# A fixed order from the z products into the SSD chunks, and an opening with two loads moved and one rounding on another engine

## The chip, the core and the metric

The kernel runs on one NeuronCore of a Trainium2 chip. The core has TensorE (PE, the matmuls), VectorE (DVE), ScalarE (ACT), GpSimd (POOL) and SyncE (SP, which here only issues DMA transfers). Each engine takes its own instructions in the order in which they stand in its queue, and waits on semaphores for the others. Data lie in SBUF, matmul results in eight PSUM banks. The metric is the device time of one execution, in microseconds (us); lower is better.

## What is computed

One layer of a hybrid encoder over 1024 tokens of width 1024, all in float32 (cut from the reference):

```
h = rmsnorm(x, norm_mix_w) * (1 + sc_m) + sh_m          # sc_m, sh_m, ... = c_act @ w_ada + b_ada
z, xbc, dt_raw, q, k, v = split(h @ w_in)
xbc = silu(causal_dwconv(xbc) + b);  xs, bm, cm = split(xbc)
dt = softplus(dt_raw + dt_bias);  A = -exp(a_log)
y_ssd = ssd_scan(xs * dt, dt * A, bm, cm) + d_skip * xs  # 8 heads, states carried over chunks
y_ssd = rmsnorm(y_ssd * silu(z), ssd_norm_w)
y_att = chunk_attention(q, k, v, rel_bias)
x = x + g_m * (concat[y_ssd, y_att] @ w_out)
h = rmsnorm(x, norm_ffn_w) * (1 + sc_f) + sh_f
x = x + g_f * ((silu(g) * v) @ w_down)                   # g, v = causal_dwconv(h @ w_up)
out = rmsnorm(x, final_norm_w)
```

## The kernel before

Every float32 operand of a large product is split into a high part, rounded to the matmul's format, and a low part, the rest: `split` writes the high part on ACT and the low part on DVE (lines 80 to 86). A product is then three matmuls, high by high, high by low and low by high (`mm3`, lines 75 to 78).

**Who sets the order.** The program text gives dependences; a planner that simulates the timeline puts the instructions of each engine in an order and assigns buffers. Three things bind it. `tc.issue_after(i)` puts an instruction behind `i` on its engine. `InOrder` (line 43) wraps VectorE, ScalarE and TensorE as `V`, `A` and `T`: while `.on` is set, each instruction goes behind the one before it, in program order. `pe` (line 683) chains TensorE's instructions of the SSD in the same way. GpSimd and the DMA queue are not wrapped.

**The opening** (lines 264 to 348). SP issues four x tiles of 128 tokens (line 267). `norm1` squares a tile on ACT, takes the root on POOL and scales it on DVE. For each of eight blocks `kt` of the model width, `mod_col` (line 131) loads a block of `w_ada` twice, for the scale and the shift, and reduces it on DVE (line 134). TensorE transposes the block of four x tiles (line 327), ACT applies scale and shift (line 249, tile `hf`), and `h_block` takes the high part (line 250) and the low part (line 251) on DVE. Products with the first columns of `w_in` follow (`first_qk`, `first_v`). The four x tiles of the second half come later, in blocks 3 to 6.

**The z products** (lines 731 to 770). z and `dt_raw` are computed in two halves of 260 columns, `ch` 1 and then 0. A half has four weight chunks of two blocks each (`wz_weights`, tiles `wzh` and `wzl`; four buffers, so that a chunk of the second half is split when the first half has left its buffer, and the last two chunks are loaded after the first two are split). Per token tile `st`, `z_tile` does 24 matmuls into a PSUM bank and evacuates it with a tanh on ACT (line 643) and a product on DVE (line 644). Tiles 0 and 1 of each four use the single banks `acc` and `pv`, tiles 2 and 3 the two-bank tiles `s`.

Beside the second half stand `dt_prep` (dt, then cumulative sums on TensorE, line 673), the splits of the output projection's weights (`wout_split`, eight slots, behind the two instructions in `pin`), and `ssd_pre(0)`, the preparation of the first SSD chunk: `xdt` and `xdd` (x times dt, lines 694 and 695), `rm` (lines 701 to 707), the segment sums `sg` on TensorE, `cb` (line 720), and the decay masks, called `th` in the trace (lines 726 and 727).

**The SSD chunks** (lines 921 to 934). The PSUM pools of the z stage are closed and new ones opened over the same eight banks. Per chunk `c` of 128 tokens, `ssd_y` issues `ydp`, `yop` (not in chunk 0) and `stp` on TensorE, `ssd_turn` transposes the y of the chunk before, `ssd_pre` prepares the next chunk, and `wout_half` does half of the output projection of a token tile (tile `wops`, with the left operand `yhl`). Everything on TensorE stands in the order of the text.

Of the kernel before, what the change touches and what calls it, by code (L numbers as in the profile page):

```python
# [64 lines left out]
def tile_block(ctx: ExitStack, tc: tile.TileContext, x, crep, pk, w_ada, w_first, w_ft, w_z,  # L65
# [182 lines left out]
    def h_block(tps, a, b, kt, hi, lo, tmp):  # L248
        i = A.activation(tmp, tps, AF.Identity, scale=a[:, kt:kt + 1], bias=b[:, kt:kt + 1])
        V.tensor_copy(hi, c4(tmp))  # L250
        return i.ins, V.tensor_tensor(lo, c4(tmp), f32(hi), ALU.subtract).ins
# [12 lines left out]
    for p in (0, 1):  # L264
        new_pair(p)
    for st in range(4):
        nc.sync.dma_start(xts[st], x[st * P:(st + 1) * P, :])

# [9 lines left out]
    adw = wu.tile([P, 2, 1024], F32, tag="w2", bufs=1, name="adat2")  # L278
# [24 lines left out]
    for hh in range(2):  # L303
# [7 lines left out]
        for kt in range(KT):  # L311
            if hh == 0:
                mod_col(SC_M + kt, wu.tile([P, 1024], F32, tag="wh", name="adat"))
                mod_scale(amix, SC_M, NMIX, kt)
                mod_col(SH_M + kt, adw[:, kt % 2, :])
                mod_shift(bmix, SH_M, kt)
                t = raw_tile(768)
                nc.sync.dma_start(t, w_first[kt])
                split(wsh[:, kt, :], ws_lo(kt), t, A, V)
                for st in range(4, NT):  # L320
                    if XL[st - 4] == kt:
                        V.tensor_copy(xts[st][:, 0:1], amix[:, kt:kt + 1])
                        nc.sync.dma_start(xts[st], x[st * P:(st + 1) * P, :])
                        norm1(st)
            tps = tp_.pop() if tp_ else ps0.tile([P, 512], F32, tag="tp0", bufs=2, name="tp0")
            for j in range(4):
                T.transpose(tps[:, j * P:(j + 1) * P], xts[4 * hh + j][:, kt * P:(kt + 1) * P], ident)
            tmp = s0.tile([P, 512], F32, tag="hf", bufs=2, name="hf")
            hi, lo = ht(hh, kt)
            pin_ = h_block(tps, amix, bmix, kt, hi, lo, tmp)  # L330
            if kt == split_at - 1:
                hpin = pin_
# [270 lines left out]
    def wout_split(slot, t):  # L603
        dh, j = WORDER[slot]
        h, l = (n[slot // 4][:, slot % 4].rearrange("p a b -> p (a b)") for n in (hth, htl))
        with tc.issue_after(pin[0]), tc.issue_after(pin[1]):
            if j < 2:
                split(h, l, t, A, V)
            else:
                for b in range(2):  # L610
                    c = slice(512 * b, 512 * b + 512)
                    k = SNW + order[2 * j + b]
                    split(h[:, c], l[:, c], t[:, c], A, V, scale=pkt[:, k:k + 1])
        ws[dh] += [(h[:, k:k + 512], l[:, k:k + 512]) for k in (0, 512)]
# [17 lines left out]
    def z_tile(ch, st, wz):  # L632
        if st % 4 < 2:
            ps = psv.tile([P, 512], F32, tag=("acc", "pv")[st % 4], bufs=1, name="zps")[:, 0:260]
        else:
            ps = s_tile()[:, 0:260]
        for kt in range(KT):
            mm3(ps, hth[st // 4][:, st % 4, kt, :], htl[st // 4][:, st % 4, kt, :],
                wz[kt // 2][0][:, kt % 2, :],
                wz[kt // 2][1][:, kt % 2, :], kt == 0, kt == KT - 1)  # L640
        nz = 260
# [4 lines left out]
        if ch == 1:  # L646
            V.scalar_tensor_tensor(zs[:, st, 512:520], ps[:, 252:260], 2.0,
                                   pkt[:, DTB:DTB + 8], op0=ALU.mult, op1=ALU.add)

    def dt_prep():  # L650
# [19 lines left out]
        pin[:] = [i.ins for i in split(adh, adl, sm["adt"], A, V)]  # L670
# [19 lines left out]
    def ssd_pre(c, xp_, sgp_, between=None):  # L690
        cs = slice(c * P, (c + 1) * P)
# [3 lines left out]
        G.tensor_tensor(h8(xdd), h8(xdt), hb("de", c), ALU.mult)  # L695
        ms_ = []
        for g in range(2):
            rm = bcp.tile([P, 2, 4, P], F32R, tag="rm", bufs=2, name="rm")
            hs = slice(c * 8 + 4 * g, c * 8 + 4 * g + 4)
            for h in range(4):  # L700
                A.activation(rm[:, 0, h, :], tle, AF.Copy, scale=f32(adh)[:, hs.start + h:hs.start + h + 1])
            if g == 0:
                V.tensor_tensor(rm[:, 1], tle.unsqueeze(1).to_broadcast([P, 4, P]),
                                f32(adl)[:, hs].unsqueeze(2).to_broadcast([P, 4, P]), ALU.mult)
            else:
                for h in range(4):
                    A.activation(rm[:, 1, h, :], tle, AF.Copy,
                                 scale=f32(adl)[:, hs.start + h:hs.start + h + 1])
            sg = sgp_()
            for i in range(2):  # L710
                pe(T.matmul, sg, sgtr, rm[:, i].rearrange("p h l -> p (h l)"), start=i == 0, stop=i == 1)
            if g == 0:
                cbp = xp_()
                for i in range(2):
                    pe(T.matmul, cbp[:, i * P:(i + 1) * P], bt_[i][:, cs], ct_[i][:, cs],
                       start=True, stop=True)
                for i in range(2):
                    pe(T.transpose, cbp[:, (2 + i) * P:(3 + i) * P], bt_[i][:, cs], ident)
                cb = bcp.tile([P, 4, P], F32, tag="cb", bufs=1, name="cb")
                V.tensor_tensor(cb.rearrange("p (a b) l -> p a b l", a=2),  # L720
                                cbp.rearrange("p (a b l) -> p a b l", a=2, b=2),
                                tle1.unsqueeze(2).to_broadcast([P, 2, 2, P]), ALU.mult)
                if between:
                    between()
            m = th512().rearrange("p (h l) -> p h l", h=4)
            pin1 = A.activation(m, sg.rearrange("p (h l) -> p h l", h=4), AF.Exp)
            pin2 = V.tensor_tensor(m, m, cb[:, g:g + 1, :].to_broadcast([P, 4, P]), ALU.mult)
            ms_.append(m)
        pin[:] = [pin1.ins, pin2.ins]
# [26 lines left out]
    for st in range(NT):  # L756
        z_tile(0, st, wz)
        if st == 0:
            wout_fold(wt[5])
            dt_prep()  # L760
        if st == 3:
            for j in (0, 1, 2):
                wout_split(j, wt[j])
            wout_get(3, 6, 7)
            pre0 = ssd_pre(0, tp_tile, tp_tile)
            wout_split(3, wt[3])
        if st >= 4:
            wout_split(st, wt[st])
# [730 lines left out]
```

## Time and profile before

| | us |
|---|---|
| median of three runs | 1224.24 |
| the runs | 1222.4, 1224.24, 1224.29 |
| the profiled execution | 1223.35 |
| its span, first to last instruction | 1221.6 |
| mean granted TensorE clock | 0.989 |

The profile is taken from one execution. In its timeline a line gives the start (us from the span's start), the duration, the engine, the program line, the operation, what it writes and reads, the shapes, the count of merged instructions, and in brackets the idle time of the engine before it with what ended that. Matmuls overlap, so their spacing is read from the starts. The granted clock is TensorE's, as a share of full speed. A wait for several semaphores is put down to the one that came last.

### The profile page before, as it was taken

How to read it: one execution, taken by the hardware profiler on the slowest of the kernel's cores; microseconds unless marked ns; L12 is line 12 of the kernel's file. 1: busy time of each engine (PE TensorE's matmuls, PEld its weight loads, DVE VectorE, ACT ScalarE, POOL GpSimd, SP SyncE). 2: the span in 40 equal slices, each digit the busy share in tenths (PEclk: the TensorE clock that was granted, in tenths of full speed). 3: DMA queues.
4: the chain of work that ended last, by engine and by line, in shares of the span. 5: the costliest groups of instructions: out<-in, count | busy, mean ns of one | idle time of the engine just before them, and what ended most of it. 6: DMA issues, size and time to landing. Idle time of an engine off the chain costs nothing.

```text
span 1221.6 us, 15652 instructions
## 1 busy us (share of the span) xinstructions
PE 1162.5 (95%) x5802; PEld 977.8 (80%) x5802; DVE 945.3 (77%) x1421; ACT 590.4 (48%) x993; POOL 198.3 (16%) x174
## 2 busy tenths in 40 slices
PE   5999999989999789999899999999999999999995
PEld 3887888778889778888688888888888888888884
DVE  7856555598797858746899988988889869766976
ACT  4537465663333646676454443444434445433443
POOL 1209373682210124300000000000000000000002
PEclk9999999999999989999999999999999999999998
DMA  9632121323554201141123223232232277733533
GB/s 341 249 94 82 36 74 39 128 89 118 175 171 169 91 9 44 53 146 61 69 78 129 94 105 129 90 100 95 104 129 97 90 280 281 270 114 125 169 119 137
DMA packets 56683, 151.91 MB, mean 124 GB/s; under 512 B 5664, under 2 KB 5792, under 8 KB 55200
## 3 DMA queue, kind: packets, MB, share of 16 engines
q1 hardware_dynamic: 49552, 126.54, 31.0%
q10 hardware_dynamic: 7056, 24.38, 5.0%
q8 instruction: 45, 0.74, 0.3%
q14 instruction: 30, 0.25, 0.1%
HBM read 117.61 MB, written 29.10 MB: 120 GB/s over the span
## 4 chain that ended last, share of the span: by engine, by line
PE 81%; DVE 11%; ACT 3%; DMA 2%; issue 2%; POOL 0%; SPq 0%; DVEq 0%; POOLq 0%; ACTq 0%
PE wops L686 6%; PE dn L77 6%; PE dn L76 6%; PE dn L78 6%; PE uY L76 5%; PE uY L78 5%; PE uY L77 5%; PE uZ L78 3%; PE uZ L76 3%; PE uZ L77 3%; PE uX L78 3%; PE uX L76 3%; PE uX L77 3%; PE acc L76 2%; PE acc L77 2%; PE acc L78 2%
## 5 line engine op out<-in xcount | busy, mean ns | idle before, releaser
L918 POOL TENSOR_TENSOR st<-st,mhalf 128x1 f32<-128x1 f32 x16 | 12.7, 799 | 691.9 <-DVE st L917 680.5
L76 PE MATMUL dn<-w 128*128 128x512 f32 x308 | 111.9, 389 | 0.0
L77 PE MATMUL dn<-w 128*128 128x512 f32 x308 | 111.9, 389 | 0.0
L78 PE MATMUL dn<-w 128*128 128x512 f32 x308 | 103.3, 389 | 0.0
L76 PE MATMUL uY<-tH,w 128*128 128x512 f32 x256 | 99.7, 389 | 1.8 <-ACT w L58 1.8
L401 POOL TENSOR_SCALAR p<-p,st 128x640 f32<-128x640 f32 (+4 forms) x64 | 98.8, 1562 | 14.4 <-DVE st L400 9.7
L77 PE MATMUL uY<-tL,w 128*128 128x512 f32 x256 | 99.6, 389 | 0.0
L78 PE MATMUL uY<-tH,w 128*128 128x512 f32 x256 | 99.6, 389 | 0.0
L85 ACT ACTIVATE w<-ya 128x1024 fp32r<-128x1024 f32 (+1 forms) x41 | 39.1, 954 | 84.8 <-PE uY L78 80.8
L686 PE MATMUL wops<-hH,yhl 128*128 128x512 f32 x224 | 74.8, 402 | 3.5 <-DVE yhl L86 2.1
L76 PEld LDWEIGHTS dn<-w 128*128 128x128 f32 x308 | 57.8, 188 | 12.1
L78 PEld LDWEIGHTS dn<-w 128*128 128x128 f32 x308 | 57.8, 188 | 12.0
L77 PEld LDWEIGHTS dn<-w 128*128 128x128 f32 x308 | 57.8, 188 | 11.9
L395 DVE CUSTOM_DVE_ANT_0 p<-s,bias 128x640 f32<-128x640 f32 (+4 forms) x64 | 40.6, 649 | 25.3 <-PE s L383 11.0
L86 DVE TENSOR_TENSOR pt<-tp,pt 128x512 fp32r<-128x512 f32 (+2 forms) x72 | 41.6, 595 | 22.2 <-ACT pt L85 13.5
L76 PEld LDWEIGHTS uY<-tH,w 128*128 128x128 f32 x256 | 48.0, 188 | 12.1 <-ACT w L58 2.2
L77 PEld LDWEIGHTS uY<-tL,w 128*128 128x128 f32 x256 | 48.0, 188 | 10.0
L78 PEld LDWEIGHTS uY<-tH,w 128*128 128x128 f32 x256 | 48.1, 188 | 10.0
L85 ACT ACTIVATE pt<-tp 128x512 fp32r<-128x512 f32 (+2 forms) x72 | 36.3, 523 | 38.8 <-PE pv L438 16.6
L85 ACT ACTIVATE w<-xs 128x1024 fp32r<-128x1024 f32 (+1 forms) x41 | 39.0, 952 | 32.4 <-PE uY L78 32.4
L686 PEld LDWEIGHTS wops<-hH,yhl 128*128 128x128 f32 x224 | 42.4, 190 | 12.8 <-DVE yhl L86 2.5
L76 PE MATMUL s<-hH,wh 128*128 128x512 f32 x128 | 50.5, 394 | 1.2 <-DVE ct L506 1.1
(445 smaller groups left out, 3427.1 us busy)
## 6 DMA issues: line engine op xcount, KB each, us to landing
gz<-a ACTq DMA_DIRECT2D x10, 1024.0 KB, 5.3
wos<-in_w_ada_dram SPq DMA_DIRECT2D x18, 512.0 KB, 4.0
ya<-in_w_up_dram SPq DMA_DIRECT2D x11, 768.0 KB, 4.2
xs<-in_w_up_dram SPq DMA_DIRECT2D x11, 768.0 KB, 4.3
adat<-in_w_ada_dram SPq DMA_DIRECT2D x16, 512.0 KB, 5.8
raws<-in_w_ft_dram SPq DMA_DIRECT2D x16, 512.0 KB, 3.6
qk<-in_w_ada_dram SPq DMA_DIRECT2D x14, 512.0 KB, 4.7
gy<-a ACTq DMA_DIRECT2D x10, 512.0 KB, 2.6
```

Source lines behind the costliest of these rows:

```text
L76: T.matmul(ps, lh, rh, start=start, stop=False, skip_group_check=more)
L77: T.matmul(ps, lh, rl, start=False, stop=False, skip_group_check=more)
L78: T.matmul(ps, ll, rh, start=False, stop=stop, skip_group_check=more)
L85: i = A.activation(hi, src, AF.Copy) if ehi is A else ehi.tensor_copy(hi, src)
L86: return i, elo.tensor_tensor(lo, src, f32(hi), ALU.subtract)
L395: V.tensor_tensor_reduce(out=dst, in0=src, in1=bsl, scale=-1.0, scalar=3e38, op0=ALU.add, op1=ALU.min, accum_out=nm)
L401: G.tensor_scalar(pv_, pv_, rr, None, op0=ALU.mult)
L686: i = op(*a, **k)
L918: G.tensor_tensor(r, ms, mhalf[:, 0:1], ALU.pow)
```

## The change

There are two parts. In the opening, the first scale and shift blocks of `w_ada` are loaded between the second and the third x tile. For the first half of the tokens the high part of h is written by ACT and no longer by DVE. The reduction of the second scale block goes behind the first low part on DVE.

In the second half of the z products `V`, `A` and `T` are set to program order, and the text is an order written by hand: a z tile's matmuls, its evacuation, and pieces of `dt_prep` (now with a separate `dt_sums`), `ssd_pre(0)` (cut into `pre_x`, `pre_rm`, `pre_sg`, `pre_cb` and `pre_m`) and `wout_split` between them. `wout_split` loses its tie to `pin`. `pre_x` and `pre_rm` of chunk 1 are written there too. Tiles 0 and 1 of each four now use `s`, tiles 2 and 3 `acc` and `pv`, in both halves. `T.on` lasts to the last z tile, whose last matmul heads the SSD's chain; `V.on` and `A.on` last through `ssd_y` of chunk 0.

```diff
-    def mod_col(ft, t, at=None):
-        nc.sync.dma_start(t, w_ada[ft])
+    def mod_col(ft, t, at=None, loaded=False):
+        if not loaded:
+            nc.sync.dma_start(t, w_ada[ft])
...
-    def h_block(tps, a, b, kt, hi, lo, tmp):
+    def h_block(tps, a, b, kt, hi, lo, tmp, ehi):
         i = A.activation(tmp, tps, AF.Identity, scale=a[:, kt:kt + 1], bias=b[:, kt:kt + 1])
-        V.tensor_copy(hi, c4(tmp))
+        if ehi is A:
+            i = A.activation(hi, c4(tmp), AF.Copy)
+        else:
+            V.tensor_copy(hi, c4(tmp))
         return i.ins, V.tensor_tensor(lo, c4(tmp), f32(hi), ALU.subtract).ins
...
     for st in range(4):
         nc.sync.dma_start(xts[st], x[st * P:(st + 1) * P, :])
+        if st == 1:
+            nc.sync.dma_start(ad0[0], w_ada[SC_M])
+            nc.sync.dma_start(ad0[1], w_ada[SH_M])
...
-                mod_col(SC_M + kt, wu.tile([P, 1024], F32, tag="wh", name="adat"))
+                t = wu.tile([P, 1024], F32, tag="wh", name="adat") if kt else ad0[0]
+                mod_col(SC_M + kt, t, low[1] if kt == 1 else None, loaded=kt == 0)
...
-                mod_col(SH_M + kt, adw[:, kt % 2, :])
+                mod_col(SH_M + kt, adw[:, kt % 2, :], loaded=kt == 0)
...
-            pin_ = h_block(tps, amix, bmix, kt, hi, lo, tmp)
+            low = h_block(tps, amix, bmix, kt, hi, lo, tmp, (A, V)[hh])
...
-    def z_tile(ch, st, wz):
-        if st % 4 < 2:
-            ps = psv.tile([P, 512], F32, tag=("acc", "pv")[st % 4], bufs=1, name="zps")[:, 0:260]
+    def z_mm(ch, st, wz):
+        if st % 4 > 1:
+            ps = psv.tile([P, 512], F32, tag=("acc", "pv")[st % 4 - 2], bufs=1, name="zps")[:, 0:260]
         else:
             ps = s_tile()[:, 0:260]
...
+    def pre_rm(c, g):
+        rm = bcp.tile([P, 2, 4, P], F32R, tag="rm", bufs=2, name="rm")
+        hs = slice(c * 8 + 4 * g, c * 8 + 4 * g + 4)
+        for h in range(4):
+            A.activation(rm[:, 0, h, :], tle, AF.Copy, scale=f32(adh)[:, hs.start + h:hs.start + h + 1])
+        if g == 0:
+            V.tensor_tensor(rm[:, 1], tle.unsqueeze(1).to_broadcast([P, 4, P]),
+                            f32(adl)[:, hs].unsqueeze(2).to_broadcast([P, 4, P]), ALU.mult)
+        else:
+            for h in range(4):
+                A.activation(rm[:, 1, h, :], tle, AF.Copy,
+                             scale=f32(adl)[:, hs.start + h:hs.start + h + 1])
+        return rm
...
-    for st in range(NT):
-        z_tile(0, st, wz)
-        if st == 0:
-            wout_fold(wt[5])
-            dt_prep()
-        if st == 3:
-            for j in (0, 1, 2):
-                wout_split(j, wt[j])
-            wout_get(3, 6, 7)
-            pre0 = ssd_pre(0, tp_tile, tp_tile)
-            wout_split(3, wt[3])
-        if st >= 4:
-            wout_split(st, wt[st])
+    V.on = A.on = T.on = True
+    V.last = A.last = T.last = None
+    zp = z_mm(0, 0, wz)
+    dt_prep()
+    z_evac(0, 0, zp)
+    zp = z_mm(0, 1, wz)
+    r0 = pre_rm(0, 0)
+    dt_sums()
+    x0 = pre_x(0)
+    z_evac(0, 1, zp)
+    wout_split(0, wt[0])
+    zp = z_mm(0, 2, wz)
+    r1 = pre_rm(0, 1)
+    g0 = pre_sg(r0, tp_tile())
+    z_evac(0, 2, zp)
+    zp = z_mm(0, 3, wz)
+    cb = pre_cb(0, tp_tile())
+    m0 = pre_m(0, g0, cb)
+    wout_fold(wt[5])
+    wout_split(1, wt[1])
+    z_evac(0, 3, zp)
+    zp = z_mm(0, 4, wz)
+    g1 = pre_sg(r1, tp_tile())
+    wout_split(2, wt[2])
+    wout_get(3, 6, 7)
+    m1 = pre_m(1, g1, cb)
+    pre0 = *x0, cb, [m0, m1]
+    z_evac(0, 4, zp)
+    zp = z_mm(0, 5, wz)
+    pre1 = {g: pre_rm(1, g) for g in range(2)}
+    pre1["x"] = pre_x(1)
+    z_evac(0, 5, zp)
+    zp = z_mm(0, 6, wz)
+    wout_split(3, wt[3])
+    wout_split(4, wt[4])
+    z_evac(0, 6, zp)
+    zp = z_mm(0, 7, wz)
+    wout_split(5, wt[5])
+    z_evac(0, 7, zp)
+    for j in (6, 7):
+        wout_split(j, wt[j])
...
     pre, turn = pre0, None
-    chain[:] = [None]
+    T.on = False
+    chain[:] = [T.last]
     for c in range(NT):
         y = ssd_y(c, *pre)
+        V.on = A.on = False
...
-            pre = ssd_pre(c + 1, x_tile, sg_tile, lambda: wout_half(c, slice(0, 3)))
+            pre = ssd_pre(c + 1, x_tile, sg_tile, lambda: wout_half(c, slice(0, 3)),
+                          pre1 if c == 0 else None)
```

More of the change, by code (lines that the diff above doesn't have):

```diff
@@ L605, in wout_split @@
         h, l = (n[slot // 4][:, slot % 4].rearrange("p a b -> p (a b)") for n in (hth, htl))
[L606 to L613, printed above, removed]
+        if j < 2:
+            split(h, l, t, A, V)
+        else:
+            for b in range(2):
+                c = slice(512 * b, 512 * b + 512)
+                k = SNW + order[2 * j + b]
+                split(h[:, c], l[:, c], t[:, c], A, V, scale=pkt[:, k:k + 1])
         ws[dh] += [(h[:, k:k + 512], l[:, k:k + 512]) for k in (0, 512)]
@@ L669, in dt_prep, with dt_sums @@
                                na.unsqueeze(1).to_broadcast([P, 8, 8]), op0=ALU.mult, op1=ALU.mult)
-        pin[:] = [i.ins for i in split(adh, adl, sm["adt"], A, V)]
+        split(adh, adl, sm["adt"], A, V)
+    def dt_sums():
         dps = tp_tile()
@@ new lines, in pre_sg, with pre_cb @@
+    def pre_sg(rm, sg):
+        for i in range(2):
+            pe(T.matmul, sg, sgtr, rm[:, i].rearrange("p h l -> p (h l)"), start=i == 0, stop=i == 1)
+        return sg
+    def pre_cb(c, cbp):
+        cs = slice(c * P, (c + 1) * P)
+        for i in range(2):
+            pe(T.matmul, cbp[:, i * P:(i + 1) * P], bt_[i][:, cs], ct_[i][:, cs],
+               start=True, stop=True)
+        for i in range(2):
+            pe(T.transpose, cbp[:, (2 + i) * P:(3 + i) * P], bt_[i][:, cs], ident)
+        cb = bcp.tile([P, 4, P], F32, tag="cb", bufs=1, name="cb")
+        V.tensor_tensor(cb.rearrange("p (a b) l -> p a b l", a=2),
+                        cbp.rearrange("p (a b l) -> p a b l", a=2, b=2),
+                        tle1.unsqueeze(2).to_broadcast([P, 2, 2, P]), ALU.mult)
+        return cb
@@ L696, in ssd_pre, with pre_m @@
+    def pre_m(g, sg, cb):
+        m = th512().rearrange("p (h l) -> p h l", h=4)
+        pin1 = A.activation(m, sg.rearrange("p (h l) -> p h l", h=4), AF.Exp)
+        pin2 = V.tensor_tensor(m, m, cb[:, g:g + 1, :].to_broadcast([P, 4, P]), ALU.mult)
+        pin[:] = [pin1.ins, pin2.ins]
+        return m
+    def ssd_pre(c, xp_, sgp_, between=None, early=None):
+        xdt, xdd = early["x"] if early else pre_x(c)
         ms_ = []
         for g in range(2):
-            rm = bcp.tile([P, 2, 4, P], F32R, tag="rm", bufs=2, name="rm")
@@ L709, in ssd_pre @@
[L709 to L722, printed above, removed]
+                cb = pre_cb(c, xp_())
```

30 lines of the change are left out of this document (12 added, 18 removed).

## The prediction

> **What bounds the kernel now.** I read the page's busy shares first, then TensorE's waits, then busy time by stretch, then the timeline on both sides of the longest wait.
>
> ```profile
> PE 1162.5 (95%) x5802; PEld 977.8 (80%) x5802; DVE 945.3 (77%) x1421; ACT 590.4 (48%) x993; POOL 198.3 (16%) x174
> ...
> PE ydp L686 <- DVE zs L644: 6.5, 1, 6.5
> ```
>
> TensorE (PE) is the bound over the whole span; only the places where it waits can be won. The longest single wait behind the opening is 6.5 us, ahead of the first SSD product (`ydp`), put down to the evacuation of the last z tile on VectorE (DVE).
>
> ```profile
> 395.10:420.60 25.50, 25.49 (x210) 25.09 (x208) 20.28 (x42) 16.14 (x39) 2.54 (x3) 1.00 0.39 125
> 420.60:427.07 6.47, 0.00 (x0) 0.00 (x0) 6.42 (x9) 5.39 (x15) 2.55 (x2) 0.67 0.00 0
> 427.07:440.00 12.93, 12.93 (x57) 11.37 (x58) 5.16 (x7) 6.04 (x18) 3.70 (x4) 0.77 0.00 1
> ...
> 427.07 3.68 PE L686 MATMUL ydp<-xdt,th 128*128 128x64 f32 x16 [6.48 <-DVE zs L644]
> 439.77 1.89 PE L686 MATMUL ydp<-xdt,th 128*128 128x64 f32 x16
> ...
> 426.61 0.41 DVE L644 SCALAR_TENSOR_TENSOR zs<-zt,s 128x260 f32<-128x260 f32 x1
> ```
>
> The first three rows are stretches: length, then PE, weight loads, DVE, ScalarE (ACT) and POOL busy (instructions), granted clock, DMA share, GB/s. In the second half of the z products PE works 25.49 of 25.50 us. Then it stands still while DVE works on (6.42 of 6.47), and behind that the granted clock is 0.77, so chunk 0 takes 12.70 us (427.07 to 439.77). DVE does the weight splits of the output projection before the last two evacuations; PE needs only the evacuations.
>
> **The z products to chunk 1, part by part.** What chunk 0 costs at full clock follows from a later chunk:
>
> ```profile
> 456.50 1.89 PE L686 MATMUL ydp<-xdt,th 128*128 128x64 f32 x16
> 458.23 1.08 PE L686 MATMUL yop<-state,ct 128*128 128x256 f32 x4
> 459.15 1.03 PE L686 MATMUL stp<-xdd,cb 128*128 128x256 f32 x4
> 460.01 0.60 PE L686 MATMUL xps<-ident,yy 128*128 128x128 f32 x4
> 460.37 0.70 PE L686 MATMUL sg<-rm,sgtr 128*128 128x512 f32 x2
> ...
> 467.50 0.66 PE L686 MATMUL ydp<-xdt,th 128*128 128x64 f32 x5
> ```
>
> Chunk 2 lasts 467.50 - 456.50 = 11.00 us. Chunk 0 has neither the `yop` product (459.15 - 458.23 = 0.92) nor the turn of an earlier y (460.37 - 460.01 = 0.36): 9.72 us.
>
> The change moves the z stage's PE work and adds none: 25.50 us. What it removes is the cover of one wait. `z_mm(0, 0)` is now in program order, while its last weights come late:
>
> ```profile
> 395.10 0.40 PE L76 MATMUL zps<-wzh,hH 128*128 128x260 f32 x2
> ...
> 397.16 0.64 ACT L82 ACTIVATE wzh<-raws 128x520 fp32r<-128x520 f32 x1 [1.48 <-DMA raws<-in_w_z_dram]
> ...
> 399.02 0.70 DVE L83 SCALAR_TENSOR_TENSOR wzl<-raws,wzh 128x520 fp32r<-128x520 f32 x1 [0.38 <-ACT wzh L82]
> ...
> 408.38 0.28 PE L76 MATMUL zps<-wzh,hH 128*128 128x260 f32 x1
> 408.50 0.28 PE L77 MATMUL zps<-wzl,hH 128*128 128x260 f32 x1
> ```
>
> Matmuls follow each other at 0.12 us, a z tile of 24 takes 2.88 us. The fourth weight chunk is split at 399.72; five matmuls come behind it, so the first tile ends near 400.32 instead of 395.10 + 2.88 = 397.98. **Added wait: 2.35 us**, in three pieces (for the third chunk's high part at 397.80, its low part some 0.7 later, the fourth's low part; the longest about 1.3). Today three tiles are mixed there, hiding it. The whole PE queue stands behind that matmul.
>
> Does `dt_sums`, second in the new order, wait as well?
>
> ```profile
> 398.45 0.18 DVE L656 TENSOR_SCALAR sm_t<-sm_e 128x64 f32<-128x64 f32 x1
> 405.63 0.23 DVE L667 SCALAR_TENSOR_TENSOR sm_e<-sm_dt,na 128x64 f32<-128x64 f32 x1
> ```
>
> This chain of fifteen small operations takes 7.4 us today because a weight split, two evacuations and a fold stand between its steps. Fifteen at 0.23 and the split at 0.70 are 4.2 us, so it ends near 403, where the second tile ends too (400.32 + 2.88). I take 0; the bounds are 0 and 2.7 (today's end).
>
> DVE and ACT get no more work, only another order. DVE's is 20.28 + 6.42 = 26.7 us, so from 395.1 it cannot end before 421.8. Following the new queue with the durations of the rows, each evacuation waiting for the tanh on ACT and that for its tile, I get its last split at about 427, today's end; the two last splits now stand behind the last evacuation, and POOL's operations beside them cost up to 1.6 us more (0.743 against 1.132 us a split, four times):
>
> ```profile
> L83 DVE SCALAR_TENSOR_TENSOR hL<-raws,pkt,hH 128x512 fp32r<-128x512 f32 x4 | 4.4, 1132 | 0.0
> ...
> L83 DVE SCALAR_TENSOR_TENSOR hL<-wos,pkt,hH 128x512 fp32r<-128x512 f32 x4 | 2.9, 743 | 0.0
> ...
> 438.05 0.69 DVE L727 TENSOR_TENSOR th<-th,cb 128x512 f32<-128x512 f32 x1 [2.02 <-ACT th L726]
> ```
>
> What is late next? `ydp` of chunk 0 needs masks made, by the same walk, near 417 and, with z tiles 6 and 7 in the two small banks, a bank that tile 5 left near 420. Chunk 1 needs its last mask (today 438.05). Behind DVE's tail stand two y operations, `cb` and two masks, 3.4 us by the 0.69 us row: 430.4, or 432.0 with POOL's share. PE asks at 395.10 + 25.50 + 2.35 + 9.72 = **432.67**. So nothing is added (bounds 0 and 1 us). The loads for slots 3, 6 and 7 stay behind the first three splits on SP's queue; they land while DMA is nearly idle and are used last.
>
> **Gain: 439.77 - 432.67 = 7.1 us.** Chunk 1's own wait stays: it comes from the turn of chunk 0's y, whose place in PE's queue does not change.
>
> **The opening.** PE starts its products when the high part of the first h block is there:
>
> ```profile
> 8.14 1.06 ACT L246 ACTIVATE junk<-qk 128x1024 f32<-128x1024 f32 x1 [0.33 <-DMA qk<-in_x_dram]
> 10.30 0.75 DVE L274 TENSOR_SCALAR qk<-qk,st 128x1024 f32<-128x1024 f32 x1 [0.75 <-POOL st L117]
> 10.73 1.06 ACT L246 ACTIVATE junk<-qk 128x1024 f32<-128x1024 f32 x1 [0.15 <-DMA qk<-in_x_dram]
> 14.15 0.75 DVE L274 TENSOR_SCALAR qk<-qk,st 128x1024 f32<-128x1024 f32 x1 [0.44 <-POOL st L117]
> 16.41 0.78 ACT L249 ACTIVATE hf<-tp,bmix,amix 128x512 f32<-128x512 f32 x1 [1.35 <-DVE bmix L209]
> 18.25 0.42 DVE L250 CAST hH<-hf 128x512 fp32r<-128x512 f32 x1
> 18.73 2.07 PE L76 MATMUL acc<-hH,wsh 128*128 128x512 f32 x4 [0.37 <-DVE hH L250]
> 50.12 0.38 PE L58 MATMUL vps<-wsh,hH 128*128 128x256 f32 x1 [0.44 <-DVE hH L250]
> ...
> 18.73:30.00 11.27, 11.27 (x54) 9.82 (x55) 11.27 (x27) 3.20 (x4) 0.00 (x0) 1.00 0.94 340
> 445.77 0.62 ACT L85 ACTIVATE yhl<-xs 128x512 fp32r<-128x512 f32 x1
> ```
>
> x tiles land 1.3 us apart (8.14 to 10.73 for two). Two loads put ahead of the last two x tiles move x3 from 10.7 to 13.3. Its norm then ends between 16.2 (as x1's: 11.05 - 8.14 = 2.9) and 17.5 (as today's x3: 14.90 - 10.73 = 4.2). Transposes (0.7), h (0.8) and ACT's rounding (0.62) follow, nothing waits for the modulation any more: 18.3 to 19.6 against 18.73, a gain of 0.4 or a loss of 0.9. I take the gain, since DVE has little beside it at 14 to 16 us. From there PE has no gap (11.27 of 11.27), so the 8 x 0.42 us taken off DVE buy nothing in the middle, only some of the 0.44 us of wait at 50; I take 0.3. ACT has room (3.20 of 11.27). **Gain: 0.7** (bounds +0.8, -0.9).
>
> **Sum:** 7.1 + 0.7 = 7.8 us off the profiled execution's 1223.35 (span 1221.6): 1215.5. The median of the runs shown is 0.9 above that execution, so **1216.4**. The rest of the program is PE-bound and only moves up.
>
> **The rivals.** The wait in the first tile may lower the clock:
>
> ```profile
> 427.07:433.00 5.93, 5.92 (x22) 5.47 (x23) 1.89 (x3) 0.40 (x1) 0.01 (x1) 0.50 0.00 0
> ...
> 446.44 0.50 PE L686 MATMUL wops<-hH,yhl 128*128 128x512 f32 x1 [1.44 <-ACT yhl L85]
> 449.27 0.73 PE L686 MATMUL wops<-hH,yhl 128*128 128x512 f32 x2 [2.10 <-DVE yhl L86]
> 449.27:456.50 7.23, 7.23 (x25) 5.75 (x25) 2.44 (x4) 4.27 (x12) 0.90 (x2) 0.76 0.10 36
> ```
>
> **Clock (chance 0.14).** In chunk 1 two waits, 1.44 and 2.10 us with two matmuls between, were followed by a mean clock of 0.76 over 7.23 us: 1.7 us lost. After the long gap it was 0.50 for 5.93 us: 3.0 lost. The new wait has smaller pieces and more matmuls between them, so I hold it less likely than not. Price 1.7 to 3.0: **1218.1 to 1219.4**.
>
> The Trainium skill, "TensorE: Matmul & The Clock Gate", Part 1, says the gate halves the clock after an idle window of about 3.4 us and restores it after as long a busy one. By that rule pieces of 1.3 us cost nothing and the sum stays at 1216.4, where chunk 1's row would make it 1218.1 or more. This case's rows disagree with a strict reading: neither of chunk 1's gaps is that long, and 5.93 us of work had not restored the clock.
>
> **Order in the other z half (0.13).** `z_mm` swaps banks for the first half too: its second tile now takes the large bank that the last conv still reads.
>
> ```profile
> 373.53 0.28 PE L76 MATMUL s<-wzh,hH 128*128 128x260 f32 x1
> ...
> 373.75 1.28 DVE L506 SCALAR_TENSOR_TENSOR xst<-s,pkt,xst 128x1021 f32<-128x1021 f32 x1
> ```
>
> The read ends at 375.0; second place comes at 373.53 - 2.88 = 370.65, third at 373.53. The planner is free there and can put tiles 2 and 3 first. If not, 1.5 to 4.4 us: **1217.9 to 1220.8**.
>
> **The release doesn't move (0.10).** If `ydp`'s bank is one of the last tile's after all, PE waits until DVE's end less the two last splits (four at 0.74): about 424.0, or 427 beside POOL. Minus 1.1 to 4.1 us: **1217.5 to 1220.5**.
>
> **Chunk 1's waits go too (0.08).** If DVE reaches the `yhl` split sooner, 1.44 + 2.10 us and the 1.7 of slow clock can go, half or all: **1211.2 to 1213.8**.
>
> **Slower (0.05).** DVE's hand-made queue becomes the bound: each evacuation waits for a tanh that stands behind splits on ACT. Each us by which DVE's tail passes 429 stops PE for one us in front of chunk 1; the gain is gone at 437. That needs 10 us of idle on DVE beyond my 427, 1.3 us a tile. Beyond it, by 2.2 us a tile: **1226 or more**. Against it: ACT is busy 16.14 of 25.50 us.
>
> **How the numbers follow.** The forecast has 0.50, between 1215 and 1218. Its neighbours reach 1211 and 1221; the ends left out are the full gain of chunk 1 and the slow case: 1212.8 to 1221.0. A measurement of this kernel can tell 0.2%, 2.4 us, from no change. Faster: 0.50 + 0.08 and most of the three middle rivals (0.37; 0.08 of it, where two of them come together, falls within 0.2%) = 0.87; same 0.08; slower 0.05.
>
> **What would show it.** Right: `ydp` of chunk 0 follows the last z matmul with no wait and at clock 1.00; a wait of about 2.4 us in the first z tile of the second half; `ydp` of chunk 1 about 7 us earlier than today, counted from the start of that half; the first h product at 18.3. Wrong: a PE wait ahead of chunk 1's `ydp` on a mask, a tile of the first half waiting for the last conv, or half clock behind 400.

## The result and the profile after

The changed kernel takes **1217.67 us** (median of 5 runs, 1215.2 to 1218.57) against 1224.24 (median of 5, 1222.4 to 1224.45): ratio 0.9947, 95% interval 0.9932 to 0.9961. The profiled execution took 1217.67 us too (span 1215.9), 5.7 less than the one before. The forecast was 1216.4.

TensorE does the same work; what has changed are its waits and the clock behind them. The page's busy line, then TensorE's timeline at each SSD chunk (start, length, what it computes; in brackets the idle time before it and what ended that):

```profile
PE 1162.3 (96%) x5802; PEld 976.8 (80%) x5802; DVE 942.3 (77%) x1413; ACT 594.9 (49%) x1001; POOL 195.2 (16%) x174
```
```profile
366.37 0.28 PE L76 MATMUL s<-wzh,hH 128*128 128x260 f32 x1
...
394.58 0.28 PE L58 MATMUL s<-wzh,hH 128*128 128x260 f32 x1
...
397.30 0.39 PE L58 MATMUL s<-wzh,hH 128*128 128x260 f32 x1 [1.11 <-ACT wzh L82]
398.04 0.39 PE L58 MATMUL s<-wzl,hH 128*128 128x260 f32 x1 [0.35 <-DVE wzl L83]
...
423.69 1.89 PE L702 MATMUL ydp<-xdt,th 128*128 128x64 f32 x16
434.01 2.00 PE L702 MATMUL ydp<-xdt,th 128*128 128x64 f32 x16 [0.43 <-DVE th L748]
438.96 0.66 PE L702 MATMUL xps<-ident,yy 128*128 128x128 f32 x4 [1.16 <-ACT yy L58]
442.18 0.50 PE L702 MATMUL wops<-hH,yhl 128*128 128x512 f32 x1 [1.42 <-ACT yhl L85]
444.06 1.22 PE L702 MATMUL wops<-hH,yhl 128*128 128x512 f32 x2 [1.15 <-DVE yhl L86]
451.00 1.22 PE L702 MATMUL ydp<-xdt,th 128*128 128x64 f32 x10
```

The wait of 6.48 us ahead of chunk 0's `ydp` is gone. New are the waits of the first z tile (397.30, 398.04), one of 0.43 for chunk 1's masks and one of 1.16 for the first y. Chunk 2's `ydp` comes at 451.00 instead of 456.50, 5.5 us sooner, and the rest of the program moves up by that.

Where TensorE's clock fell is read from the busy time by stretch (length, PE, weight loads, DVE, ACT, POOL busy with their instructions, granted clock, DMA share, GB/s):

```profile
395.73:399.14 3.41, 1.93 (x12) 1.31 (x11) 1.98 (x6) 1.52 (x4) 0.00 (x0) 1.00 0.28 95
399.14:402.55 3.41, 3.41 (x16) 3.41 (x17) 2.96 (x14) 0.00 (x0) 0.00 (x0) 0.50 0.91 301
402.55:405.96 3.41, 3.41 (x31) 3.41 (x30) 2.42 (x6) 2.69 (x9) 0.58 (x1) 1.00 0.03 11
```

Behind the first tile's waits PE ran 3.41 us at half clock: 16 matmuls where the next 3.41 us hold 31.

### The profile page after: what moved, and what is told of

It is laid out like the page before. It is cut to its first block, busy times and chain, and to the rows that moved or that the text cites. A ratio compares the mean times of both kernels' runs of the same rounds, so it can differ in the third digit from the quotient of the medians.

```text
span 1215.9 us, 15656 instructions
## 1 busy us (share of the span) xinstructions
PE 1162.3 (96%) x5802; PEld 976.8 (80%) x5802; DVE 942.3 (77%) x1413; ACT 594.9 (49%) x1001; POOL 195.2 (16%) x174
## 4 chain that ended last, share of the span: by engine, by line
PE 67%; DVE 7%; ACT 2%; DMA 1%; issue 1%; POOL 0%; DVEq 0%; POOLq 0%; SPq 0%; ACTq 0%
PE dn L76 6%; PE dn L77 6%; PE dn L78 6%; PE wops L702 6%; PE uY L76 5%; PE uY L78 5%; PE uY L77 5%; PE uZ L78 3%; PE uZ L77 3%; PE uZ L76 3%; PE uX L78 3%; PE uX L77 3%; PE uX L76 3%; PE s L76 2%; PE s L77 2%; PE s L78 2%
```

## The experiments

Two theories to begin with. **A:** `ydp` of chunk 0 came free because the z tiles swapped banks; VectorE's tail of weight splits then sets chunk 1; and the half clock behind the first tile costs another 1.7 us. **B:** the fixed order of VectorE and ScalarE is what does it, and TensorE alone sets chunk 1. Each run had five rounds beside the kernel before, whose median in these sessions lay between 1224.05 and 1225.67, so ratios are compared. The stage is read from one profiled execution of each kernel. Since what comes ahead of the z products differs by up to 3.8 us from one of these to another (their start lies at 366.4 to 370.2), the stage is counted from its own start, the first z matmul:

| kernel | z start to chunk 0's ydp | chunk 0 | chunk 1 | sum | ratio to before, 95% interval |
|---|---|---|---|---|---|
| before | 60.17 | 12.70 | 16.73 | 89.60 | 1 |
| changed | 57.32 | 10.32 | 16.99 | 84.63 | 0.9947 (0.9932 to 0.9961) |
| opening alone | 60.17 | 13.24 | 16.72 | 90.13 | 0.9999 (0.9988 to 1.0011) |
| order and swap, old opening | 56.07 | 10.32 | 18.41 | 84.80 | 0.9950 (0.9934 to 0.9965) |
| order, old banks | 61.02 | 13.04 | 16.69 | 90.75 | 0.9992 (0.9981 to 1.0004) |
| swap alone | 53.54 | 13.42 | 16.63 | 83.59 | 0.9945 (0.9929 to 0.9962) |
| first tiles mixed | 54.55 | 11.58 | 18.48 | 84.61 | 0.9946 (0.9932 to 0.9960) |
| late splits, free | 56.01 | 11.65 | 20.73 | 88.39 | 0.9996 (0.9986 to 1.0006) |
| both of these | 54.59 | 12.31 | 20.07 | 86.97 | 0.9981 (0.9969 to 0.9992) |
| late splits, bound | 57.44 | 9.72 | 13.89 | 81.05 | 0.9924 (0.9909 to 0.9939) |
| and turn ahead of ydp | 57.09 | 14.76 | 14.48 | 86.33 | 0.9962 (0.9946 to 0.9979) |
| bound and mixed | 54.12 | 9.73 | 16.71 | 80.56 | 0.9915 (0.9898 to 0.9931) |
| and turn behind ydp | 54.51 | 9.73 | 19.91 | 84.15 | 0.9951 (0.9939 to 0.9964) |
| and splits behind yhl | 54.14 | 9.73 | 13.58 | 77.45 | 0.9908 (0.9892 to 0.9923) |

### Which part does it: banks or order

The changed kernel with the old banks, and the kernel before with the new ones:

```diff
-        if st % 4 > 1:
-            ps = psv.tile([P, 512], F32, tag=("acc", "pv")[st % 4 - 2], bufs=1, name="zps")[:, 0:260]
+        if st % 4 < 2:
+            ps = psv.tile([P, 512], F32, tag=("acc", "pv")[st % 4], bufs=1, name="zps")[:, 0:260]
```

(the second run is this read backwards, in `z_tile` of the kernel before).

> The changed kernel with the banks of the z tiles as before the change (tiles 0, 1, 4, 5 in the small banks, 2, 3, 6, 7 in the large ones), order unchanged. Theory 1 (the swap of banks is what lets chunk 0's ydp go ahead of the last evacuation): ydp of chunk 0 waits for the evacuation of the last tile, at about 427.2 instead of 423.7, idle 3.5 us, clock below 1.00 behind it: ydp of chunk 1 3 to 6 us later, time 1220.5 to 1223.5. Theory 2 (the order by itself does it: the splits no longer stand before the evacuations): ydp of chunk 0 loses less than 1 us, time 1217 to 1218.5.

> The kernel before with the swap of the z tiles' banks alone: no order by hand, opening as before. With the changed order but the old banks the time was that of before (ratio 0.9992). If the swap alone frees ydp's bank, ydp of chunk 0 comes when the tile two or more before the last is evacuated, and most of the gain is there: 1218 to 1220 against 1224.2. If both are needed (in the planner's order VectorE does the splits ahead of the evacuations of tiles 4 and 5 too, and of the masks), the wait of 6.5 us shrinks by less than 2 us: 1222.5 to 1225.

The order with the old banks is worth nothing that can be told (0.9992, interval 0.9981 to 1.0004); the swap alone is worth the whole gain (0.9945, against 0.9947). TensorE's timeline, first of the order with the old banks, then of the swap alone:

```profile
428.75 3.68 PE L702 MATMUL ydp<-xdt,th 128*128 128x64 f32 x16 [3.39 <-DVE zs L58]
```
```profile
421.07 1.89 PE L686 MATMUL ydp<-xdt,th 128*128 128x64 f32 x16
426.16 0.71 PE L686 MATMUL xps<-ct,bt 128*128 128x128 f32 x4 [1.81 <-DVE zs L644]
434.49 1.90 PE L686 MATMUL ydp<-xdt,th 128*128 128x64 f32 x16
```

And VectorE in the swap alone, where the last two evacuations stand (`zs`):

```profile
415.68 0.43 DVE L644 SCALAR_TENSOR_TENSOR zs<-zt,s 128x260 f32<-128x260 f32 x1 [0.51 <-ACT zt L643]
...
425.69 0.41 DVE L644 SCALAR_TENSOR_TENSOR zs<-zt,zps 128x260 f32<-128x260 f32 x1
...
429.25 0.41 DVE L644 SCALAR_TENSOR_TENSOR zs<-zt,zps 128x260 f32<-128x260 f32 x1
```

With the old banks `ydp` waits for the last evacuation even though the splits of slots 6 and 7 now stand behind it. With the new ones it starts at 421.07, while two evacuations are still to come (425.69 and 429.25): its bank was left by 415.68, the last evacuation of a tile `s`. So banks, not order, hold or free it. What the order then does is a trade. It takes away the wait of 1.81 us for the bank of z tile 6 inside chunk 0 and the clock lost behind it (chunk 0: 13.42 to 10.32, 3.1 us), and it pays 2.5 to 3.8 us in the z products (53.54 against 56.07 and 57.32), where the planner mixes tiles so that no wait shows. The two about cancel.

### The opening

On the kernel before, the first six hunks of the diff alone: the two loads behind x1, the rounding and the pin.

```diff
+        if st == 1:
+            nc.sync.dma_start(ad0[0], w_ada[SC_M])
+            nc.sync.dma_start(ad0[1], w_ada[SH_M])
...
+        if ehi is A:
+            i = A.activation(hi, c4(tmp), AF.Copy)
```

The second run is the changed kernel with these undone.

> The kernel before with the opening's part of the change alone (two loads moved, the high part rounded on ScalarE, the pin). As forecast: first h product at 18.3, 0.7 us off: 1223.5. Rival, from the trace of the changed kernel (the third stretch at 50 us starts as late as before, the convolution 0.13 us sooner): 0 to 0.3 us off, 1223.9 to 1224.3. Both lie within what a comparison of times can tell; the starts in the trace decide.

> The changed kernel with the opening as before: the order from the z products on alone. The whole measured gain less 0 to 0.7 us: 1217.7 to 1218.4; counted from the start of the second z half, ydp of chunk 1 comes 38.2 to 39.5 us later (44.7 before). Whether the clock falls behind the first tile's waits in this run is open: with the same waits (1.11 and 0.35 us) it fell for 3.4 us in the changed kernel and did not in the run with late splits. If it is a matter of where a waiting time falls against a fixed beat, it may go either way here; if the waits alone decide, it falls.

Neither comparison of times shows the opening (0.9999; and 0.9950 without it against 0.9947 with it). In the trace of the opening alone:

```profile
17.80 1.12 PE L336 MATMUL tp<-ident,qk 128*128 128x128 f32 x4 [0.66 <-ACT hf L250]
...
50.32 0.39 PE L58 MATMUL vps<-wsh,hH 128*128 128x256 f32 x1 [0.54 <-ACT hH L252]
51.04 0.39 PE L58 MATMUL vps<-wsh,hL 128*128 128x256 f32 x1 [0.22 <-DVE hL L255]
```

The wait at 50 us does not go. It is now for ScalarE, 0.54 us here and 0.39 in the changed kernel's trace, against 0.44 before, and the product behind it starts at 50.12 before and at 50.13 in the changed kernel. Counted from the first transpose, the first h product comes at 9.12, 9.12 and 9.59 us in the three traces with the old opening and at 8.66 to 9.23 (mean 8.95) in eleven with the new: about 0.3 us, less than one trace differs from the next. In the changed kernel's own trace it starts at 18.32, as forecast. In the second run the first tile waited 0.98 and 0.35 us and the clock did not fall, so the waits alone do not decide that.

### The first tile's waits and VectorE's tail

Three edits of the changed kernel: the first three z tiles mixed; the last two splits (slots 6 and 7) written behind chunk 1's preparation, in the loop behind `wout_half(c, slice(3, 8))`, and left to the planner; both. Mixed (`z_kt` is the loop over `kt` of `z_mm`; the rests of tiles 1 and 2 follow in the same way):

```diff
-    zp = z_mm(0, 0, wz)
+    z3 = [z_mm(0, st, wz, range(4)) for st in range(3)]
+    z_kt(0, wz, z3[0], range(4, KT))
```

Late, free:

```diff
-    for j in (6, 7):
-        wout_split(j, wt[j])
...
+            if c == 0:
+                for j in (6, 7):
+                    wout_split(j, wt[j])
```

> The changed kernel, with the first three z tiles of the second half mixed by hand: products of the first two weight chunks for tiles 0, 1 and 2, then the rest of each. Covers the wait of the first tile for weight chunks 3 and 4. Both theories: no wait in the z products behind 394.6 and no half clock behind 398.9, so chunk 0's ydp comes 3.0 to 3.5 us sooner (1.46 of waits named, some 1.7 of slow clock) than 29.1 us after the half began. Theory 1 (VectorE's tail sets chunk 1): the masks for chunk 1 stay at about 434.0, so PE's gain turns into a longer wait there, 0.43 becomes 3 to 4 us, with a clock that falls behind it: time 1217.0 to 1219.0, no gain. Theory 2 (PE alone sets it): chunk 1 also comes 3 us sooner: 1214.2 to 1214.7.

> The changed kernel, with the last two weight splits (slots 6 and 7, first read in chunk 2) written behind chunk 1's preparation and left to the planner; z order unchanged. VectorE's tail behind the last evacuation loses four splits (4 x 0.73 to 1.1 us). Theory 1 (VectorE's tail sets chunk 1): the mask wait of 0.43 us ends, the first y is made 3 us or more sooner, the wait of 1.16 us for it in the turn ends, and of the two waits for yhl (1.42 and 1.15) at least one goes, and with them the clock loss of chunk 1: ydp of chunk 2 comes 2 to 5 us sooner, time 1213 to 1216. Theory 2 (the turn's waits come from the order of PE and ScalarE, not from VectorE's tail): only 0.4 us, time 1217.2.

> Both edits together: first three z tiles mixed, last two splits late. Theory 1: the two gains, which hide each other alone, add up: chunk 0's ydp 3.0 to 3.5 us sooner and chunk 1 after it without a mask wait; time 3.3 us below that with the late splits alone, 1210 to 1213. Theory 2 (chunk 1's waits have nothing to do with VectorE's tail): 1214.

(These texts call chunk 2 the first reader of the two slots; it is the second half of the output products in chunk 1's turn of the loop.) The mixed tiles gave TensorE 2.8 us (57.32 to 54.55) and the time did not move, 0.9946: chunk 0 grew by 1.3 us and chunk 1 by 1.5. TensorE in that run:

```profile
433.64 2.68 PE L705 MATMUL ydp<-xdt,th 128*128 128x64 f32 x16 [1.70 <-DVE th L751]
```

The wait for the masks grew from 0.43 to 1.70, as A said, though not to the 3 to 4 us written: 0.77 us of the lead went to a wait for the dt chain inside the z products, which the text had not expected, and the clock fell behind the masks (half clock from 434.77 to 438.18). Behind TensorE, VectorE was already the next bound.

The free splits were a miss, alone and with the mixed tiles (1224.38 and 1222.45 us, where 1213 to 1216 and 1210 to 1213 were expected). VectorE's timeline in the run with the splits alone, then two rows of ScalarE:

```profile
426.42 1.54 DVE L83 SCALAR_TENSOR_TENSOR hL<-raws,pkt,hH 128x512 fp32r<-128x512 f32 x1
427.88 1.53 DVE L719 TENSOR_TENSOR rm<-tle,adl 128x512 fp32r<-128x512 f32 x1
429.33 1.53 DVE L83 SCALAR_TENSOR_TENSOR hL<-raws,pkt,hH 128x512 fp32r<-128x512 f32 x1
430.78 0.41 DVE L58 SCALAR_TENSOR_TENSOR zs<-zt,zps 128x260 f32<-128x260 f32 x1
...
436.93 0.69 DVE L748 TENSOR_TENSOR th<-th,cb 128x512 f32<-128x512 f32 x1 [2.47 <-ACT th L747]
```
```profile
435.69 0.72 ACT L58 ACTIVATE yy<-yy,st 128x512 f32<-128x512 f32 x1 [1.01 <-POOL st L117]
436.32 0.58 ACT L747 ACTIVATE th<-sg 128x512 f32<-128x512 f32 x1
```

Lines L83 are the late splits, L58 the work in fixed order. The planner, free to place them, put them in the gaps of the fixed order, ahead of the last evacuation (430.78 instead of 426.78). It moved something else too: the exponential of the second mask now stands on ScalarE behind the scaling of the first y (436.32; in the changed kernel it comes at 430.20, ahead of that y), so the second mask came at 436.93 and TensorE waited twice in chunk 1's `ydp`, 1.76 and 2.05 us. So the experiment did not do what it was meant to; the next one binds the splits.

### The late splits bound, and the turn of the first y

At the same place, bound behind chunk 1's last mask; and for the second run the turn added behind them, ahead of chunk 1's `ydp`:

```diff
+            if c == 0:
+                with tc.issue_after(pin[0]), tc.issue_after(pin[1]):
+                    for j in (6, 7):
+                        wout_split(j, wt[j])
```
```diff
+                ssd_turn(*turn)
+                turn = None
```

> The changed kernel, with the last two weight splits (slots 6 and 7) behind the masks of chunk 1, bound there so that the planner cannot bring them forward (in the run with late splits left free it put them ahead of the last evacuation). Theory 1 (VectorE's and ScalarE's tail delays the masks and the first y): chunk 1's ydp has no mask wait (0.43 now), the transposes of the first y wait less than 0.3 us (1.16 now); the two waits for yhl (1.42 and 1.15) stay, since their chain begins at those transposes: 1.5 to 2.0 us off, 1215.7 to 1216.2. Theory 2 (the waits move on to what comes next on VectorE): the yhl wait grows by as much, 1217.2 to 1218.2.

> As the run before, and the turn of the first y (four transposes and the copy back) ahead of chunk 1's ydp instead of behind its stp. If the waits for yhl in chunk 1 come from the short way from the turn to the products that read it, they go (1.42 + 1.15 us, and the clock loss behind them, 1.3 to 1.7 us), at the price of a wait for the first y in the turn of 0 to 1.5 us: 1211.5 to 1214. If they come from VectorE's queue instead, they stay and the time is that of the run before, 1215.7 to 1218.

Bound, they gain: 0.9924. TensorE in that run:

```profile
424.93 1.89 PE L702 MATMUL ydp<-xdt,th 128*128 128x64 f32 x16
434.65 1.89 PE L702 MATMUL ydp<-xdt,th 128*128 128x64 f32 x16
438.78 0.66 PE L702 MATMUL xps<-ident,yy 128*128 128x128 f32 x4 [0.45 <-ACT yy L58]
441.99 0.50 PE L702 MATMUL wops<-hH,yhl 128*128 128x512 f32 x1 [1.44 <-ACT yhl L85]
442.93 0.73 PE L702 MATMUL wops<-hH,yhl 128*128 128x512 f32 x2 [0.20 <-DVE yhl L86]
```

No mask wait, chunk 0 in 9.72 us; the wait for the first y went from 1.16 to 0.45, that for the low part of `yhl` from 1.15 to 0.20, and the clock stayed at 1.00 through chunk 1, 3.6 us in this stage in all. Theory A holds with a larger effect than written: the wait for the low part nearly went too, since VectorE had worked off what stood in front of it and began the low part at 441.97, as soon as the high part was there.

The early turn was a miss in its price: 4 us, not 0 to 1.5. TensorE, then ScalarE in that run:

```profile
438.74 1.11 PE L702 MATMUL xps<-ident,yy 128*128 128x128 f32 x4 [3.96 <-ACT yy L58]
```
```profile
431.89 1.33 ACT L82 ACTIVATE hH<-wos,pkt 128x512 fp32r<-128x512 f32 x2
433.12 1.33 ACT L82 ACTIVATE hH<-raws,pkt 128x512 fp32r<-128x512 f32 x2
434.35 1.27 ACT L717 ACTIVATE rm<-tle,adh 128x128 fp32r<-128x128 f32 x4
435.52 0.39 ACT L723 ACTIVATE rm<-tle,adl 128x128 fp32r<-128x128 f32 x1
435.81 0.62 ACT L58 ACTIVATE yt<-yy 128x512 f32<-128x512 f32 x1
```

The waits for `yhl` did go, but the square of the first y (435.81) stands behind the late splits' high parts and the masks' factors on ScalarE. VectorE had that y ready at 433.93, so this queue accounts for 1.9 of the 3.96 us; the rest is the way from the y to the turn itself (square, root on GpSimd, scaling, done at 438.7), which by itself is more than the price allowed. ScalarE's queue is the part that can be cleared.

### Both gains together

Bound and mixed is the two edits above, with `dt_sums` and `pre_x(0)` behind the third tile. The next run adds the turn between chunk 1's `ydp` and `yop`, and binds the splits behind `ypin`, the scaling of the first y:

```diff
+        if mid:
+            mid()
...
-        y = ssd_y(c, *pre)
+        y = ssd_y(c, *pre, mid=(lambda: ssd_turn(*turn)) if c == 1 else None)
...
-                with tc.issue_after(pin[0]), tc.issue_after(pin[1]):
+                with tc.issue_after(pin[1]), tc.issue_after(ypin):
```

The last moves them into `wout_half`, behind the high part of `yhl`:

```diff
-                wout_rhs(q // 2, q % 2)
+                r = wout_rhs(q // 2, q % 2)
+                if q == 1:
+                    with tc.issue_after(r[0].ins):
+                        for j in (6, 7):
+                            wout_split(j, wt[j])
```

> The changed kernel with the bound late splits, the first three z tiles mixed by hand and the sums of dt one tile later (in the run that mixed them alone they waited 0.8 us for the dt chain). Theory 1 (each of the two gains was hidden by the other's wait): ydp of chunk 0 comes 25.5 to 26.3 us after the half began (29.1 in the changed kernel) and chunk 1 follows without a mask wait: 2 to 3.5 us below the run with the bound splits alone. Theory 2 (VectorE's tail is full even then, since it works without a pause from 420 to 442): the lead of 2 to 3 us at chunk 0 is given back at the masks and at the first y of chunk 1, at most 1 us below that run.

> The run with bound late splits and mixed tiles, with the turn of the first y between chunk 1's ydp and yop (ahead of the ydp, without the mixed tiles, it waited 4.0 us for the first y), and the late splits bound behind the scaling of that y on ScalarE, so that ScalarE no longer does 2.7 us of splits ahead of the y's square. Theory 1 (the waits of 1.44 and 1.86 us for yhl in chunk 1 are the length of the chain from the turn to the split, 2 us of which the earlier turn covers): together 0.5 to 1.5 us are left of 3.3, and the clock holds or not as the beat of 3.41 us falls: 1.5 to 4 us below that run, 1210.8 to 1213.3. Theory 2 (ScalarE's queue sets them): the wait moves to the turn, no gain.

> As the run before, with the late splits one place further back, behind the high part of yhl in chunk 1. ScalarE then goes from the scaled y to the copy back and to yhl with nothing between. Theory 1: both waits for yhl go (less than 0.5 us left of 3.3), and the clock stays at 1.00 through chunk 1: 3 to 5 us below the run with bound splits and mixed tiles, 1209.8 to 1211.8. The price, if the two splits are now too late for the second half of chunk 1's output products, is a wait of 0.5 to 2 us there.

Bound and mixed: the z products take 3.3 us less than in the run with the bound splits (57.44 to 54.12) and chunk 0 stays at 9.73; but chunk 1 takes 2.8 more (13.89 to 16.71). TensorE in that run:

```profile
438.61 0.50 PE L705 MATMUL wops<-hH,yhl 128*128 128x512 f32 x1 [1.44 <-ACT yhl L85]
441.21 0.74 PE L705 MATMUL wops<-hH,yhl 128*128 128x512 f32 x2 [1.86 <-DVE yhl L86]
```

The lead is given back at the low part of `yhl` (0.20 became 1.86) and in a stretch of half clock behind it: theory 2's size (half a us in the stage), at another place than it named. The turn behind `ydp` with the splits behind the y's scaling failed in a new place: the low parts of the late splits now stood on VectorE ahead of the low part of `yhl` (four halves between 435.02 and 440.5, and `rm`, a y operation and `cb` behind them), and TensorE waited 4.52 us for that. With the splits behind `yhl` both waits are gone, and there is no half clock from 390 to 460; what shows instead is 0.90 us for a late split and 0.44 for a mask. TensorE there:

```profile
436.19 0.66 PE L705 MATMUL xps<-ident,yy 128*128 128x128 f32 x4 [0.23 <-ACT yy L58]
...
445.78 0.50 PE L705 MATMUL wops<-hL,yhl 128*128 128x512 f32 x1 [0.90 <-DVE hL L83]
...
447.65 0.55 PE L705 MATMUL ydp<-xdt,th 128*128 128x64 f32 x3 [0.44 <-DVE th L751]
```

The stage is 3.1 us shorter than bound and mixed. The time is **1213.25 us**, ratio 0.9908 (0.9892 to 0.9923), the lowest here and clear of the changed kernel's interval; from bound and mixed (0.9915) times do not tell it apart. The time expected, 1209.8 to 1211.8, was missed; the 3.1 us in the stage are the low end of the 3 to 5 expected. Whether bound splits on top of the swap alone, without the order by hand, would do as well was not run.

## Why the prediction was right, and where it was not

**The release of chunk 0.** Right in mechanism: `ydp` follows the last z matmul with no wait and at full clock, because its bank was that of an earlier tile, and the run with the old banks shows it waiting again. The prediction named the bank, but took the change as one: it did not ask what the planner would have made of the swap by itself, so it did not see that the swap alone does it and that the fixed order adds nothing measurable.

**The added wait, 2.35 us.** Right. With late splits left free, where the clock did not fall, the half took 27.80 us from 395.07 to 422.87, 25.50 of work and 2.30 of waiting. In the changed kernel it took 29.11 (394.58 to 423.69).

**The clock.** The rival held at 0.14 came, in the execution that was profiled: 1.3 us more (29.11 - 27.80) for 3.41 us at half clock, less than the 1.7 to 3.0 put on it. The step that failed is "smaller pieces and more matmuls between them, so I hold it less likely than not". Size of the pieces does not decide. The same waits of 1.11 and 0.35 us fell as follows in the run with late splits left free:

```profile
396.92:400.33 3.41, 2.19 (x14) 1.84 (x15) 2.38 (x6) 1.52 (x4) 0.00 (x0) 1.00 0.33 102
400.33:403.75 3.42, 3.40 (x29) 3.19 (x28) 2.66 (x13) 0.49 (x3) 0.00 (x0) 1.00 0.76 252
```

Of six kernels with this order the clock fell behind the first tile in four and not in two, one trace each, so 0.14 was too little; see the last section.

**Chunk 1's masks, 0 (bounds 0 and 1).** In range: 0.43. VectorE's timeline in the changed kernel:

```profile
426.78 0.41 DVE L58 SCALAR_TENSOR_TENSOR zs<-zt,zps 128x260 f32<-128x260 f32 x1
427.12 0.68 DVE L709 TENSOR_TENSOR xdt<-xs,sm_dt 128x512 f32<-128x512 f32 x1
427.72 2.19 DVE L58 SCALAR_TENSOR_TENSOR hL<-wos,pkt,hH 128x512 fp32r<-128x512 f32 x2
429.83 1.53 DVE L719 TENSOR_TENSOR rm<-tle,adl 128x512 fp32r<-128x512 f32 x1
...
433.28 1.28 DVE L748 TENSOR_TENSOR th<-th,cb 128x512 f32<-128x512 f32 x2
...
434.64 0.68 DVE L58 TENSOR_TENSOR yy<-ydp,yy 128x512 f32<-128x512 f32 x1
```

The forecast had the masks done at 430.4 to 432.0; they were made from 433.28 to 434.56. The walk had the last split done at 427; it ended at 433.2. Two things made it late. The planner slipped work into VectorE's fixed order that the walk left out, `xdt` and `rm` of chunk 2 (0.68 and 1.53 us; `rm` takes 0.68 at 403.76, and 1.53 here, where GpSimd is busy from 429.32 to 430.81). The larger part is idle time: from 394.58 to 433.21 VectorE was busy 29.43 of 38.63 us, so it stood idle for 9.2, where the walk's 427 holds 5.2 (427 - 395.1 - 26.7). That chunk 0 costs 9.72 us when nothing is late was right: 9.72 and 9.73 in the runs with the splits bound.

**"Chunk 1's own wait stays"** was right in sum (16.99 for 16.73), but not for the reason given: 1.16 of it was new (the first y, begun at 434.64 on VectorE, 7.4 us after the last evacuation), and 0.95 less was lost at the low part of `yhl`. It does not come from the place in TensorE's queue alone: the bound splits took 3.1 us of it away.

**The opening, 0.7 us.** Mis-sized: about 0.3, by the traces; the 0.3 taken at 50 us did not come, since the rounding is as late on ScalarE as it was on VectorE.

**The other rivals.** The first half did not wait for the last conv: PE was busy 28.21 of the 28.21 us from 366.37 to 394.58. VectorE's queue did become the next bound, but cost 0.43 us at the masks and 1.16 at the first y, and not the gain. The release did move; the run with the old banks shows what it would have cost had it not: nearly the whole gain, more than the 1.1 to 4.1 us written, since the wait of 3.39 us is followed by half clock and chunk 0 takes 13.04.

**The sum.** Forecast 7.8 us off the profiled execution, measured 5.7. In the stage 7.1 were forecast at chunk 1's `ydp`, counted from the start of the second half, and 5.24 came (44.67 to 39.43): 1.26 went to the clock and 0.60 to the masks and the rest of chunk 0. The median fell by 6.6, and the forecast of 1216.4 was 1.3 us low. That the time still lies within the forecast's own 1215 to 1218, although the clock rival came, is partly luck: executions of the changed kernel alone lie between 1215.2 and 1218.57.

## What to carry to other kernels

When an engine waits for an evacuation, look first at which buffer its next tile takes: here two lines that choose the bank gave the whole gain, and some forty lines of order without them gave nothing. A fixed order helps only as far as all that can stand in it is bound: a planner fills its gaps with whatever is left free, and the same two splits, moved back, won 3.6 us of the stage when bound, while left free they ended up ahead of the last evacuation, the planner moved a mask's work back with them, and the stage grew by 3.8. And a lead won ahead of a second engine that is full is a wait there until that engine's queue is shortened too.

## What the runs showed of the hardware that was not expected

**The clock falls on a beat.** In the fourteen traces here, from 20 us to TensorE's last products, every stretch at half clock lasts 3.41, 6.83 or 10.24 us, that is one, two or three times 3.41, and within a trace the starts between 390 and 460 us lie whole multiples of 3.41 apart (399.14 and 443.51 in the changed kernel: 13.0). The kernel before, by stretch:

```profile
422.84:426.25 3.41, 0.00 (x0) 0.00 (x0) 3.41 (x6) 3.15 (x8) 0.31 (x1) 0.50 0.00 0
426.25:429.67 3.42, 2.60 (x12) 2.60 (x13) 0.77 (x2) 0.00 (x0) 0.00 (x0) 0.50 0.00 0
429.67:433.08 3.41, 3.41 (x12) 2.95 (x12) 1.89 (x3) 0.48 (x1) 0.09 (x1) 0.50 0.00 0
433.08:436.49 3.41, 3.41 (x19) 2.91 (x19) 2.58 (x3) 2.38 (x8) 3.33 (x4) 1.00 0.01 2
```

Cut along that beat between 390 and 460 us, a beat at full clock in which PE was busy 0.47 of the time or less was always followed by one at half clock, one above 0.61 never; from 0.50 to 0.61 both happened (0.57 in the changed kernel fell; 0.58 three times and 0.52 twice elsewhere did not). So one wait of 1.1 us can cost another 1.3 (the changed kernel) or nothing (late splits left free), by where it falls. That executions of one kernel differ by such steps is not shown, since one trace of each was kept. Ahead of the z products, the trace with the splits behind `yhl` has three beats at half clock, which fits its late start (370.2); the nine traces with one start them at 366.9 to 368.8, the four with none at 366.4 to 367.5. What kind of work counts as busy, and why a wholly busy beat at half clock was sometimes followed by another (429.67 was busy for 3.41 and the next was full; with the opening alone, 428.55 to 431.97 was busy throughout and the next was not), stays open.

The Trainium skill, "TensorE: Matmul & The Clock Gate", Part 1, gives a free-running window of 3413 ns; these runs agree to 0.01 us. Its table lets the clock fall after an idle window; here a window that was busy to 0.57 was enough, so the measurement decides. The prediction held 5.93 us of work at half clock against the rule on restoring; cut on the beat, the first wholly busy window there is 429.67 to 433.08, and the clock was back behind it, so that row does not speak against the rule, while the run with the opening alone does.
